# A decoder layer on one core: a front that multiplies before its norm, ten weight residues made by DMA, and a conv-out in split form throughout

## The chip, the core and the metric

The kernel runs on one core of a Trainium2 chip. The core has five engines that run beside each other and meet at semaphores: TensorE (PE in the profile; the loading of its weights, which overlaps the matmuls, is shown as PEld), VectorE (DVE), ScalarE (ACT), GpSimd (POOL) and SyncE (SP), which here only issues transfers; 16 DMA engines carry these. The metric is the device time of one execution in microseconds, lower is better.

## The reference

One layer of a trunk with sequence length 256, model width 1024, batch 1, all in float32:

```python
n = rmsnorm(x) * g_mix
z = n @ w_in                    # a, gate, q, k, v, index q, index k, index weights, two gate logits
u = a * sigmoid(gate)           # conv branch: causal depthwise convolution, 31 taps
u = causal_conv31(u) + conv_b
y_conv = silu(layernorm(u) * ln_g + ln_b) @ w_conv_out
y_attn = sparse_attention(q, k, v, index...) @ w_attn_out      # 8 heads, 64 keys of each query
h = x + (g_conv * y_conv + g_attn * y_attn) @ w_mix_out
h = h + cross_attention(rmsnorm(h), rmsnorm(mem))              # 4 heads, 256 memory tokens
h = h + square(relu(rmsnorm(h) @ w_ff1)) @ w_ff2               # width 4096
return rmsnorm(h) * g_final
```

Some 85 MB of weights pass through the core once.

## The kernel before

**Split products.** A product in float32 is made in one of two ways. *Native*: PE multiplies the float32 operands as they are, which appears in the trace as two matmul records for each matmul. *Split*: each operand is written as a high part, rounded to the type fp32r, and a low part, the rest (raw − high); three fp32r matmuls (`mm3`: high·high, high·low, low·high) replace one native product.

**The stream of weights.** The weights come in the fixed order `STREAM`, in chunks of 1 MB (128 partitions x 2048), two halves each. `load()` issues the next chunk on SP's queue into one of three `raw` buffers. For each half, `high` (line 174) has ACT copy the raw half to the high part (line 178), and its inner `low` has DVE subtract it to give the low part; when the low part of a chunk's second half is emitted, the next `load()` is issued, since the raw buffer then comes free. `highs` and `lows` have six buffers (`HALVES`). `weights(kind, i, half, kt)` hands out a prepared half; `split_ahead()`, called once for each half that is used, emits one more low part and one more high part. So the number of halves prepared ahead stays what it was. Chunks in `WHOLE` are used native and are never split: these are conv 0 and co 0. Chunks in `EARLY` have a buffer of their own: chunk 3 and co 0.

**The order** of each engine's instructions is written out by the program (a manual schedule): each engine runs its own in the order in which they were emitted. Work that is not tied to a product waits in generators (`chains`), which `tick()`, called after each half, moves on by one step each, and in `fill`, a list of taps of the convolution. `Counted` keeps a running estimate of PE's and DVE's work (`pe.total`, `dve.total`), and `tick` emits taps on DVE as long as its estimate is over 1 us behind PE's.

**The front** (lines 321 to 411). SP loads x in rows (`x_rm`, two loads), then the chunks conv 0, conv 1 and conv 2, the taps' weights `cw` and chunk 3. POOL's queue loads `vec`, a tile with all gains and biases. PE makes ten matmuls on zeros (`ps_warm`, line 350). ACT squares the rows with a sum, DVE and POOL make the scale of each row (POOL's `pow`), DVE multiplies, PE transposes to feature-major (`pt_n`), ACT and DVE multiply by the gain `g_mix` into `n_f`, and its high and low parts go to `n2`. conv 0 is native from `n_f`; everything later that takes n uses `n2`.

**The conv branch.** `conv_in(i)` makes two halves (gate and value of 128 channels), the sigmoid, the product `u`, and puts 30 taps of DVE on `fill`; `tap(t, s)` adds one. When a channel tile has its last tap, POOL adds it to `usum` (line 455), and the last of eight starts `layer_norm()` (line 595). This runs step by step at ticks: the mean over the channels by a matmul (`ps_mub`), squares, their sum (`ps_vr`), POOL's `pow`, the spread of the row scale (`ps_rsb`), then four multiplications on DVE and eight Silu on ACT over `acc`, and last the high and low parts of `acc`, two channel tiles at a tick (`parts_of`, into `u2`).

**From attention to the mix.** The products q, k, xk, xv and ao (attention out) are split; the heads run in chains. `form_b` makes one half after the other in the two banks `ps_mm`. After ao, the loop `while not normed: tick()` runs until the Silu is emitted; then co (conv out) follows. co 0 is native and reads `acc` itself, by `form_b_whole` (line 302) in two banks of `ps_acc`, in four steps with a tick behind each, during which the parts of `u2` are made; co 1 to 3 are split and use `u2`. `gated` (line 717) multiplies the result by its gate on DVE, adds the attention branch and makes the parts for mix. `form_b_late`, which other stages use, makes all but the last k tile of both halves first, then the last tile of both.

**The feed-forward.** `form_c_last("xo", ...)` ends the cross attention; `xo_residual` (line 912) makes the parts `ff_p`. Then `f1` and `f2` chunks alternate; f1 0 is made with `form_b_late`.

Line 77 is the helper through which all counted PE and DVE instructions are recorded.

Of the kernel before, what the change touches and what calls it, by code (L numbers as in the profile page):

```python
# [8 lines left out]
F32 = mybir.dt.float32  # L9
# [3 lines left out]
ALU = mybir.AluOpType  # L13
# [41 lines left out]
NK = 72  # L55
N_CHUNK = KT * S
HALVES = 6
EARLY = (3, STREAM.index(("co", 0)))
WHOLE = (("conv", 0), ("co", 0))


class Counted:
# [49 lines left out]
def block_kernel(ctx, tc, x, xt, mem, memt, wst, wki, vecs, convw, gout, out):  # L112
# [15 lines left out]
    def t8(name, dt=F32, shape=(P, KT, S)):  # L128
        return big.tile(list(shape), dt, tag="t8", bufs=12, name=name)

    def parts_t8(name, nkt=KT):
        return Parts([t8(f"{name}{c}", F32R, (P, 4, 2, S)) for c in range(nkt // 4)])
# [10 lines left out]
    def ps_acc(name):  # L143
        return bank("acc", 4, name)
# [9 lines left out]
    def load(parts=1):  # L154
        if nload[0] >= len(STREAM):
            return
        c = nload[0]
        nload[0] += 1
        key = STREAM[c]
        raw = t8(f"raw{c}", F32, (P, N_CHUNK)) if c in EARLY else raws.tile([P, N_CHUNK], F32, tag="raw", name=f"raw{c}")  # L160
        n = KT * NK if key[0] == "ki" else N_CHUNK
        src = wki if key[0] == "ki" else wst[INDEX[key]]
        for q in range(parts):
            ns = slice(q * n // parts, (q + 1) * n // parts)
            nc.sync.dma_start(raw[:, ns], src[:, ns])
        if key in WHOLE:
            whole[key] = raw.rearrange("p (k n) -> p k n", k=2 * KT)
            return
        parts = 1 if key[0] == "ki" else 2
        for q in range(parts):  # L170
            ns = slice(q * n // parts, (q + 1) * n // parts)
            high_jobs.append(lambda ns=ns, q=q, last=q == parts - 1: high(key, c, raw, ns, q, last))

    def high(key, c, raw, ns, q, last):
        n = ns.stop - ns.start
        hi = highs.tile([P, N_CHUNK // 2], F32R, tag="hi", name=f"hi{c}_{q}")[:, :n]
        lo = lows.tile([P, N_CHUNK // 2], F32R, tag="lo", name=f"lo{c}_{q}")[:, :n]
        act(hi, raw[:, ns], AF.Copy)  # L178

        def low():  # L180
            dve.tensor_tensor(out=lo, in0=raw[:, ns], in1=hi.bitcast(F32), op=ALU.subtract)
            prepared[(*key, q)] = (hi, lo)
            if last and c not in EARLY:
                load()

        low_jobs.append(low)
# [26 lines left out]
    def split_ahead():  # L213
        if not waiting[0]:
            split_low()
        split_high()

    def tick():
        for c in list(chains):
            if next(c, "end") == "end":  # L220
                chains.remove(c)
        while (len(fill) > 1 or (fill and (len(done) > 5 or nused[0] < 5))) and dve.total < pe.total - 1000:
            fill_one()
        dve.total = max(dve.total, pe.total - 2000)
# [18 lines left out]
    def split(hi, lo, src):  # L243
        act(hi, src, AF.Copy)
        dve.tensor_tensor(out=lo, in0=src, in1=hi.bitcast(F32), op=ALU.subtract)
# [53 lines left out]
            tick()  # L299
        held[0] = 1  # L300

    def form_b_whole(kind, i, x, after, cuts):

        w = whole[(kind, i)]
        banks = [ps_acc(f"ps_{kind}{i}{ct}")[:, :S] for ct in range(2)]
        for lo, hi in zip((0, *cuts), (*cuts, KT)):
            for ct in range(2):
                for kt in range(lo, hi):
                    pe.matmul(banks[ct], w[:, ct * KT + kt, :], x[:, kt, :], start=kt == 0, stop=kt == KT - 1)
            split_ahead()  # L310
            if hi == KT:
                load()
            tick()
        for ct in range(2):
            after(2 * i + ct, banks[ct])

    def copy_to(dst):
        return lambda ct, ps: act(dst[:, ct, :], ps, AF.Copy)


    x_rm = t8("x_rm", F32, (P, 2, D))
    for rb in range(2):
        nc.sync.dma_start(x_rm[:, rb, :], x[rb * P : (rb + 1) * P, :])
    vec = cst.tile([P, 72], F32, name="vec")
    nc.gpsimd.dma_start(vec, vecs)
    bgc, bga, cvb, lng, lnb, g_mix, g_mem, g_x, g_ffn = (vec[:, 8 * j : 8 * j + 8] for j in range(9))
    cw = cst.tile([P, KT, TAPS], F32, name="cw")
    for parts in (2, 2, 1):
        load(parts)
    nc.sync.dma_start(cw, convw.rearrange("p (k t) -> p k t", k=KT))  # L330
    load()
    zero = w2("zero")
    nc.vector.memset(zero, 0.0)
# [12 lines left out]
    nc.scalar.activation(half, half, AF.Sigmoid, bias=0.0, scale=0.0)  # L346
    nc.gpsimd.memset(half, -0.5)
    ps = ps_aux("ps_warm")
    for j in range(10):
        nc.tensor.matmul(ps, zero_r[:, :P], zero_r, start=True, stop=True)  # L350


# [5 lines left out]
    def row_square(src, rb, ss):  # L358
        junk = w2(f"junk_{src.name if hasattr(src, 'name') else ''}{rb}", BF16, (P, D))
        act(junk, src[:, rb, :], AF.Square, accum_out=ss[:, rb : rb + 1])  # L360
# [21 lines left out]


    n2 = parts_t8("n_p")
    n_f = t8("n_f")
    ss = small.tile([P, 2], F32, tag="ss", name="ss_n")
    ptn = [ps_acc(f"pt_n{c}") for c in range(4)]
    for rb in range(2):
        row_square(x_rm, rb, ss)
    for rb in range(2):  # L390
        ms = small.tile([P, 1], F32, tag="ms1", name=f"ms_n{rb}")
        dve.tensor_scalar(ms, ss[:, rb : rb + 1], 1.0 / D, EPS, ALU.mult, ALU.add)
        rs = small.tile([P, 1], F32, tag="rs1", name=f"rs_n{rb}")
        nc.gpsimd.tensor_tensor(out=rs, in0=ms, in1=half[:, 0:1], op=ALU.pow)
        dve.tensor_scalar(x_rm[:, rb, :], x_rm[:, rb, :], rs[:, 0:1], None, ALU.mult)
        for kt in range(KT):
            pe.transpose(ptn[kt // 2][:, (kt % 2) * S + rb * P : (kt % 2) * S + rb * P + P],
                         x_rm[:, rb, kt * P : kt * P + P], ident)
    for kt in range(KT):
        src = ptn[kt // 2][:, (kt % 2) * S : (kt % 2) * S + S]  # L400
        if kt % 2 == 1:
            dve.tensor_scalar(n_f[:, kt, :], src, g_mix[:, kt : kt + 1], None, ALU.mult)
        else:
            act(n_f[:, kt, :], src, AF.Copy, scale=g_mix[:, kt : kt + 1])
    for c in range(0, KT, 2):
        split(n2.high(c, 2), n2.low(c, 2), n_f[:, c : c + 2, :])
    split_high()
    split_low()
    split_high()
    pe.total = dve.total = 0.0  # L410


    mem2 = parts_t8("mem_p")
# [28 lines left out]
    def tap(t, s):  # L442
        def go():
            j = TAPS - 1 - s
            if s == 0:
                act(acc[:, t, :], u[:, t, :], AF.Identity, scale=cw[:, t, j : j + 1], bias=cvb[:, t : t + 1])
            else:
                dve.scalar_tensor_tensor(out=acc[:, t, s:], in0=u[:, t, : S - s], scalar=cw[:, t, j : j + 1],
                                         in1=acc[:, t, s:], op0=ALU.mult, op1=ALU.add)
            if s == TAPS - 1:  # L450
                done.append(t)
                if len(done) == KT:
                    start(layer_norm())
                if len(done) > 1:
                    nc.gpsimd.tensor_tensor(out=usum, in0=usum if len(done) > 2 else acc[:, done[0], :],
                                            in1=acc[:, t, :], op=ALU.add)
        return go

    def conv_tile(i, half):
        key = ("conv", i)  # L460
        w = weights("conv", i, half, KT) if key not in WHOLE else None
        split_ahead()
        ps = ps_mm(f"ps_conv{i}{half}")
        if w:
            tile_b(ps, w, n2)
        else:
            for kt in range(KT):
                pe.matmul(ps[:, :S], whole[key][:, half * KT + kt, :], n_f[:, kt, :], start=kt == 0, stop=kt == KT - 1)
        return ps

    def conv_in(i):
        psg = conv_tile(i, 0)
        sg = w2(f"sg{i}", F32, (P, S))
        act(sg, psg[:, :S], AF.Sigmoid)
        tick()
        psa = conv_tile(i, 1)
        dve.tensor_tensor(out=u[:, i, :], in0=psa[:, :S], in1=sg, op=ALU.mult)
        tick()
        tap(i, 0)()
        fill.append([tap(i, s) for s in range(1, TAPS)])  # L480
        if ("conv", i) in WHOLE:
            load()

    for i in range(4):
        conv_in(i)
        if i == 1:
            start(memory())


    qi_t = t8("qi_t", F32, (P, 4, S))  # L490
# [97 lines left out]
        form_a("v", hf, n2, v_rm, (1.0, 1.0))  # L588


    u2 = []

    normed = []

    def layer_norm():
        u2.append(parts_t8("u_p"))
# [25 lines left out]
        for c, cs in enumerate(pairs):  # L622
            dve.tensor_tensor(out=acc[:, cs, :], in0=acc[:, cs, :], in1=rsb, op=ALU.mult)
            for t in (2 * c, 2 * c + 1):
                act(acc[:, t, :], acc[:, t, :], AF.Silu, scale=lng[:, t : t + 1], bias=lnb[:, t : t + 1])
        normed.append(True)
        for c in range(4):
            yield
            parts_of(2 * c)
# [74 lines left out]
        form_b("ao", i, o2, copy_to(ya))  # L704
    while fill:
        fill_one()
    while not normed:
        tick()


    h_t = t8("h_t")
# [18 lines left out]

    gate_branch(0)
    for i in range(4):
        if i == 0:
            form_b_whole("co", i, acc, gated, (2, 4, 6))
        else:
            form_b("co", i, u2[0], gated)
    low_due.pop()()


# [386 lines left out]
```

## Time and profile before

| | |
|---|---|
| median of 3 runs | 516.89 us (516.72 to 516.94) |
| profiled execution | 516.86 us, its span 515.1 us |
| granted TensorE clock | 0.998 |
| PE busy | 504.3 us, 98% of the span |
| DVE, ACT, POOL busy | 419.4 us (81%), 286.9 us (56%), 19.2 us (4%) |
| DMA moved | 92.75 MB, mean 180 GB/s |

Rows of the profile read so: in a group of instructions, the line, engine and operation, out<-in with the shapes, the count, then busy time in all, mean ns of one, and the idle time of the engine before them with what ended it. In the timeline and in the chain, the first number is the start in us and the second the duration. In the list of waits: us in total, times, longest. In DMA issues: KB of each and the median time from issue to landing. `<-` in brackets names what released the waiting instruction.

### The profile page before, as it was taken

What the parts mean: (1) busy time and instruction counts of PE and PEld (TensorE: products, weight loads), DVE (VectorE), ACT (ScalarE), POOL (GpSimd) and SP (SyncE); (2) the same over time, 40 slices, a digit from 0 to 9 for tenths busy, and PEclk for the clock granted to TensorE, in tenths of its full rate; (3) what the DMA queues carried; (4) which work ended last, traced back from release to release, by engine and by line L of the source; (5) the groups of instructions that cost most, each with busy time, mean ns of one, the idle gap of its engine ahead of it and who ended that gap; (6) DMA issues with size and microseconds to landing.
All of it is one profiled execution on the core that took longest, in us unless ns stands there. A gap on an engine that the chain in (4) does not pass through costs nothing.

```text
span 515.1 us, 8515 instructions
## 1 busy us (share of the span) xinstructions
PE 504.3 (98%) x3354; PEld 463.1 (90%) x3354; DVE 419.4 (81%) x796; ACT 286.9 (56%) x489; POOL 19.2 (4%) x30
## 2 busy tenths in 40 slices
PE   7999999999999999999999999999999999999995
PEld 5999999999899999999999998988888888888884
DVE  4998999999988999999898976696766566666565
ACT  5666655546446666656655657565654454554442
POOL 2000000001001000021000000000000000000000
PEclk9999999999999999999999999999999999999999
DMA  8856435464552343454744541446445554445402
GB/s 317 359 187 236 155 122 205 174 225 183 194 216 102 144 164 118 155 224 161 275 143 155 207 184 44 181 165 242 164 169 220 221 207 163 164 174 219 181 1 81
DMA packets 14311, 92.75 MB, mean 180 GB/s; under 512 B 1584, under 2 KB 2480, under 8 KB 3776
## 3 DMA queue, kind: packets, MB, share of 16 engines
q1 hardware_dynamic: 13952, 91.85, 48.3%
q8 instruction: 26, 0.43, 0.3%
q10 hardware_dynamic: 288, 0.33, 0.2%
q14 instruction: 13, 0.11, 0.1%
q0 software_dynamic: 32, 0.04, 0.0%
HBM read 91.16 MB, written 1.05 MB: 179 GB/s over the span
## 4 chain that ended last, share of the span: by engine, by line
PE 95%; issue 1%; ACT 1%; DVE 1%; DMA 1%; POOL 0%; POOLq 0%; DVEq 0%; ACTq 0%
PE ps_f L77 17%; PE ps_ff L77 16%; PE ps_conv L77 9%; PE ps_co L77 5%; PE ps_ao L77 4%; PE ps_ga L77 4%; PE ps_gc L77 4%; PE ps_k L77 4%; PE ps_q L77 4%; PE ps_mix L77 4%; PE ps_v L77 4%; PE ps_xo L77 3%; PE ps_xq L77 2%; PE ps_qi L77 2%; PE ps_xk L77 2%; PE ps_xv L77 2%
## 5 line engine op out<-in xcount | busy, mean ns | idle before, releaser
L77 DVE TENSOR_TENSOR lo<-raw,hi 128x1024 fp32r<-128x1024 f32 x161 | 195.7, 1225 | 3.3 <-ACT hi L178 1.6
L178 ACT ACTIVATE hi<-raw 128x1024 fp32r<-128x1024 f32 x161 | 166.4, 1047 | 2.5 <-PE ps_v L77 2.5
L77 DVE SCALAR_TENSOR_TENSOR acc<-u,cw,acc 128x255 f32<-128x255 f32 (+27 forms) x240 | 100.6, 475 | 0.6
L77 PE MATMUL ps_f<-ff_p,hi 128*128 128x512 f32 x256 | 89.8, 396 | 0.0
L77 PE MATMUL ps_ff<-hi,fs 128*128 128x512 f32 (+1 forms) x256 | 80.8, 387 | 0.0
L77 PE MATMUL ps_f<-ff_p,lo 128*128 128x256 f32 x256 | 66.2, 279 | 0.0
L77 PEld LDWEIGHTS ps_ff<-hi,fs 128*128 128x128 f32 x256 | 47.9, 188 | 9.2
L77 PEld LDWEIGHTS ps_f<-ff_p,hi 128*128 128x128 f32 x256 | 46.8, 188 | 9.2
L77 DVE TENSOR_TENSOR ft<-ps_f,ft 128x256 f32<-128x256 f32 x32 | 13.6, 423 | 46.4 <-ACT ft L957 46.4
L77 PEld LDWEIGHTS ps_f<-ff_p,lo 128*128 128x128 f32 x256 | 48.2, 188 | 2.6
L957 ACT ACTIVATE ft<-ps_f 128x256 f32<-128x256 f32 x32 | 12.2, 380 | 66.9 <-PE ps_f L77 66.9
L77 PE MATMUL ps_ff<-lo,fs 128*128 128x512 f32 (+1 forms) x128 | 49.4, 386 | 0.0
L77 PE MATMUL ps_conv<-n_p,hi 128*128 128x256 f32 x224 | 41.0, 285 | 0.0
L77 PEld LDWEIGHTS ps_conv<-n_p,hi 128*128 128x128 f32 x224 | 34.9, 192 | 0.8 <-issue 0.7
L77 PE MATMUL ps_conv<-n_p,lo 128*128 128x256 f32 x112 | 31.7, 283 | 0.0
L77 PEld LDWEIGHTS ps_ff<-lo,fs 128*128 128x128 f32 x128 | 24.1, 188 | 4.9
L77 PE MATMUL ps_q<-n_p,hi 128*128 128x256 f32 x128 | 24.4, 291 | 0.0
L77 PE MATMUL ps_ao<-o_p,hi 128*128 128x256 f32 x128 | 23.5, 285 | 0.0
L77 PE MATMUL ps_k<-n_p,hi 128*128 128x256 f32 x128 | 23.4, 284 | 0.0
L77 PE MATMUL ps_gc<-n_p,hi 128*128 128x256 f32 x128 | 23.1, 283 | 0.0
L77 PE MATMUL ps_ga<-n_p,hi 128*128 128x256 f32 x128 | 23.1, 283 | 0.0
L77 PE MATMUL ps_mix<-mix_p,hi 128*128 128x512 f32 (+1 forms) x80 | 22.1, 350 | 0.0
(229 smaller groups left out, 1003.3 us busy)
## 6 DMA issues: line engine op xcount, KB each, us to landing
raw<-in_wst_dram SPq DMA_DIRECT2D x80, 1024.0 KB, 4.8
raw<-in_wst_dram SPq DMA_DIRECT2D x4, 512.0 KB, 7.7
x_rm<-in_x_dram SPq DMA_DIRECT2D x2, 512.0 KB, 3.9
mem_rm<-in_mem_dram SPq DMA_DIRECT2D x1, 1024.0 KB, 9.0
mem_t<-in_memt_dram SPq DMA_DIRECT2D x1, 1024.0 KB, 11.0
h_t<-in_xt_dram SPq DMA_DIRECT2D x1, 1024.0 KB, 6.9
out_dram<-hg SPq DMA_DIRECT2D x4, 176.0 KB, 2.2
g_out<-in_gout_dram SPq DMA_DIRECT2D x1, 512.0 KB, 7.0
```

Source lines behind the costliest of these rows:

```text
L77: return fn(*args, **kwargs)
L178: act(hi, raw[:, ns], AF.Copy)
L957: act(t, ps[:, S:], AF.Copy)
```

## The change

It has three parts.

1. **The front.** x is loaded feature-major (`x_t`, two loads of four k tiles, the second behind the first half of conv 0). `xg` is x times the gain, not yet normed: two of the eight k tiles on ACT, six on DVE. conv 0 and conv 1 are native from `xg` in four `ps_acc` banks (`conv_in_first`). The squares of x are summed on ACT and DVE; `row_scale` makes the row scale with matmuls (`ps_n`) amid conv 0, spreads it (`rsb_n`) behind conv 0, and makes the normed `n_f` and the parts `n2` on DVE and ACT. The scale is put on the results of the two native chunks afterwards: the gate is multiplied by `rsb`, goes through the sigmoid, and is multiplied by `rsb` again. `cw` is loaded behind the second chunk, not the third. The matmuls on zeros are six instead of ten, and the planner starts behind this front with `pe.total = 0` and `dve.total = 2000` where both were 0 ahead of conv 0.
2. **Ten low parts by DMA.** For the second halves of the chunks 8, 11, ... 35 (the last is ao 0), ACT writes −high to the low part and a DMA on POOL's queue adds the raw half to it, in place of DVE's subtraction.
3. **co 0 is split** like the others and uses `u2`, by `form_b_late`; `form_b_whole` goes, and the loop before co runs until the whole chain of `layer_norm`, its parts included, has been emitted.

```diff
-EARLY = (3, STREAM.index(("co", 0)))
-WHOLE = (("conv", 0), ("co", 0))
+EARLY = (3,)
+WHOLE = (("conv", 0), ("conv", 1))
...
             nc.sync.dma_start(raw[:, ns], src[:, ns])
+            if c == 0 and q == 0:
+                nc.sync.dma_start(x_t[:, 4:8, :], xt[:, 4:8, :])
...
+    def low_by_dma(key, c, q):
+        return q == 1 and c % 3 == 2 and 8 <= c < STREAM.index(("ao", 1))
...
         act(hi, raw[:, ns], AF.Copy)
+        by_dma = low_by_dma(key, c, q)
+        if by_dma:
+            act(lo, hi.bitcast(F32), AF.Copy, scale=-1.0)
 
         def low():
-            dve.tensor_tensor(out=lo, in0=raw[:, ns], in1=hi.bitcast(F32), op=ALU.subtract)
+            if by_dma:
+                nc.gpsimd.dma_start(lo.bitcast(F32), raw[:, ns], accum_op=ALU.add)
+            else:
+                dve.tensor_tensor(out=lo, in0=raw[:, ns], in1=hi.bitcast(F32), op=ALU.subtract)
...
-    x_rm = t8("x_rm", F32, (P, 2, D))
-    for rb in range(2):
-        nc.sync.dma_start(x_rm[:, rb, :], x[rb * P : (rb + 1) * P, :])
+    x_t = t8("x_t")
     vec = cst.tile([P, 72], F32, name="vec")
     nc.gpsimd.dma_start(vec, vecs)
...
-    for parts in (2, 2, 1):
+    nc.sync.dma_start(x_t[:, 0:4, :], xt[:, 0:4, :])
+    for parts in (2, 1):
         load(parts)
     nc.sync.dma_start(cw, convw.rearrange("p (k t) -> p k t", k=KT))
     load()
+    load()
...
-    for j in range(10):
+    for j in range(6):
         nc.tensor.matmul(ps, zero_r[:, :P], zero_r, start=True, stop=True)
...
+    for kt in range(KT):
+        gain(kt, None if kt in (0, 2) else dve)
+    for hf in range(2):
+        act(n_f[:, 4 * hf : 4 * hf + 4, :], x_t[:, 4 * hf : 4 * hf + 4, :], AF.Square)
+    for n in (4, 2, 1):
+        dve.tensor_tensor(out=n_f[:, :n, :], in0=n_f[:, :n, :], in1=n_f[:, n : 2 * n, :], op=ALU.add)
+
+    def row_scale():
+        rs = rsqrt(n_f[:, 0, :], "n")
+        yield
+        act(rsb, spread(rs, "rsb_n"), AF.Copy)
+        yield
+        for c in range(0, KT + 2, 2):
+            if c < KT:
+                dve.tensor_tensor(out=n_f[:, c : c + 2, :], in0=xg[:, c : c + 2, :],
+                                  in1=rsb.unsqueeze(1).to_broadcast([P, 2, S]), op=ALU.mult)
+                act(n2.high(c, 2), n_f[:, c : c + 2, :], AF.Copy)
+            if c > 0:
+                dve.tensor_tensor(out=n2.low(c - 2, 2), in0=n_f[:, c - 2 : c, :], in1=n2.high(c - 2, 2).bitcast(F32),
+                                  op=ALU.subtract)
+            if c == 2:
+                split_high()
+            if c == 4:
+                split_low()
...
+    def conv_in_first():
+        scaling, banks = row_scale(), []
+        for i in range(2):
+            for half in range(2):
+                ps = ps_acc(f"ps_conv{i}{half}")[:, :S]
+                banks.append(ps)
+                for kt in range(KT):
+                    pe.matmul(ps, whole[("conv", i)][:, half * KT + kt, :], xg[:, kt, :], start=kt == 0,
+                              stop=kt == KT - 1)
+                    if kt == KT // 2 - 1 and i == 0 and half == 1:
+                        next(scaling)
...
+        for i in range(2):
+            psg, psa = banks[2 * i : 2 * i + 2]
+            sg = w2(f"sg{i}", F32, (P, S))
+            dve.tensor_tensor(out=sg, in0=psg, in1=rsb, op=ALU.mult)
+            act(sg, sg, AF.Sigmoid)
+            dve.tensor_tensor(out=sg, in0=sg, in1=rsb, op=ALU.mult)
+            gated_linear(i, psa, sg)
+
+    conv_in_first()
+    split_low()
+    pe.total = 0.0
+    dve.total = 2000.0
...
-    while not normed:
-        tick()
+    finish(norms[0])
...
     for i in range(4):
-        if i == 0:
-            form_b_whole("co", i, acc, gated, (2, 4, 6))
-        else:
-            form_b("co", i, u2[0], gated)
+        (form_b_late if i == 0 else form_b)("co", i, u2[0], gated)
```

More of the change, by code (lines that the diff above doesn't have):

```diff
@@ L300, in form_b_late @@
         held[0] = 1
[L302 to L312, printed above, removed]
-            tick()
-        for ct in range(2):
-            after(2 * i + ct, banks[ct])
     def copy_to(dst):
         return lambda ct, ps: act(dst[:, ct, :], ps, AF.Copy)
-    x_rm = t8("x_rm", F32, (P, 2, D))
-    for rb in range(2):
-        nc.sync.dma_start(x_rm[:, rb, :], x[rb * P : (rb + 1) * P, :])
+    x_t = t8("x_t")
     vec = cst.tile([P, 72], F32, name="vec")
@@ L384, in block_kernel @@
     n2 = parts_t8("n_p")
+    xg = t8("xg")
     n_f = t8("n_f")
[L386 to L398, printed above, removed]
@@ L399, in block_kernel @@
-    for kt in range(KT):
-        src = ptn[kt // 2][:, (kt % 2) * S : (kt % 2) * S + S]
-        if kt % 2 == 1:
-            dve.tensor_scalar(n_f[:, kt, :], src, g_mix[:, kt : kt + 1], None, ALU.mult)
-        else:
[L404 to L410, printed above, removed]
+    rsb = w2("rsb", F32, (P, S))
@@ new lines, in gain @@
+    def gain(kt, engine):
+        if engine is dve:
+            dve.tensor_scalar(xg[:, kt, :], x_t[:, kt, :], g_mix[:, kt : kt + 1], None, ALU.mult)
+        else:
+            act(xg[:, kt, :], x_t[:, kt, :], AF.Copy, scale=g_mix[:, kt : kt + 1])
+    for kt in range(KT):
+        gain(kt, None if kt in (0, 2) else dve)
[3 more added lines that the diff above has]
+        dve.tensor_tensor(out=n_f[:, :n, :], in0=n_f[:, :n, :], in1=n_f[:, n : 2 * n, :], op=ALU.add)
@@ new lines, in row_scale @@
+    def row_scale():
[15 more added lines that the diff above has]
+                split_low()
+        split_high()
+        split_low()
+        split_high()
+        yield
@@ L452, in go @@
                 if len(done) == KT:
-                    start(layer_norm())
+                    norms.append(start(layer_norm()))
                 if len(done) > 1:
@@ L459, in conv_tile @@
     def conv_tile(i, half):
-        key = ("conv", i)
-        w = weights("conv", i, half, KT) if key not in WHOLE else None
+        w = weights("conv", i, half, KT)
         split_ahead()
         ps = ps_mm(f"ps_conv{i}{half}")
[L464 to L468, printed above, removed]
+        tile_b(ps, w, n2)
         return ps
@@ L476, in conv_in, with gated_linear @@
         psa = conv_tile(i, 1)
-        dve.tensor_tensor(out=u[:, i, :], in0=psa[:, :S], in1=sg, op=ALU.mult)
-        tick()
+        gated_linear(i, psa[:, :S], sg)
+    def gated_linear(i, ps, sg):
+        dve.tensor_tensor(out=u[:, i, :], in0=ps, in1=sg, op=ALU.mult)
+        if ("conv", i) not in WHOLE:
+            tick()
         tap(i, 0)()
         fill.append([tap(i, s) for s in range(1, TAPS)])
-        if ("conv", i) in WHOLE:
-            load()
-    for i in range(4):
+    def conv_in_first():
[9 more added lines that the diff above has]
+                        next(scaling)
+                if half == 1:
+                    load()
+                if i == 0 and half == 1:
+                    next(scaling)
+                    next(scaling)
+        for i in range(2):
[6 more added lines that the diff above has]
+    conv_in_first()
+    split_low()
+    pe.total = 0.0
+    dve.total = 2000.0
+    start(memory())
+    for i in range(2, 4):
         conv_in(i)
-        if i == 1:
-            start(memory())
     qi_t = t8("qi_t", F32, (P, 4, S))
@@ L588, in block_kernel @@
         form_a("v", hf, n2, v_rm, (1.0, 1.0))
-    u2 = []
-    normed = []
+    u2, norms = [], []
     def layer_norm():
@@ L625, in layer_norm @@
                 act(acc[:, t, :], acc[:, t, :], AF.Silu, scale=lng[:, t : t + 1], bias=lnb[:, t : t + 1])
-        normed.append(True)
         for c in range(4):
@@ L706, in block_kernel @@
         fill_one()
-    while not normed:
-        tick()
+    finish(norms[0])
     h_t = t8("h_t")
@@ L732, in block_kernel @@
     for i in range(4):
-        if i == 0:
-            form_b_whole("co", i, acc, gated, (2, 4, 6))
-        else:
-            form_b("co", i, u2[0], gated)
+        (form_b_late if i == 0 else form_b)("co", i, u2[0], gated)
     low_due.pop()()
```

## The prediction

> **What bounds the kernel now.** I read four views in this order: busy time by engine, PE's waits, the chain of waits in order of time, and then the timeline around each place that the change touches.
>
> ```profile
> PE 504.3 (98%) x3354; PEld 463.1 (90%) x3354; DVE 419.4 (81%) x796; ACT 286.9 (56%) x489; POOL 19.2 (4%) x30
> ```
> ```profile
> core 0 of [0], span 515.1 us
> engine line waited for: us in total, times, longest us
> PE ps_warm L350 <- DVE zero_r L335: 1.9, 1, 1.9
> PE pt_n L77 <- DVE ms_n L77: 1.3, 1, 1.3
> PE ps_xo L77 <- ACT xptr L853: 0.8, 1, 0.8
> PE pt_n L77 <- DVE x_rm L77: 0.4, 1, 0.4
> ```
>
> PE is busy 504.3 of 515.1 us, and its whole list of waits is 4.4 us, of which 3.6 (all but ps_xo's 0.8) lie ahead of the first useful matmul. So an edit pays only if it takes matmul time off PE or moves the first matmul forward, and it costs as soon as it makes PE wait. DVE at 81% and ACT at 56% are covers: work taken off them is worth nothing by itself. The profiled run took 516.86 us, 1.8 more than its span, against a median of 516.89; I sum in the span and carry the result over unchanged. Differences under 0.2%, about 1 us, can't be told from no change.
>
> **The front.**
>
> ```profile
> 0.74 3.51 DMA x_rm<-in_x_dram
> ```
> ```profile
> 1.24 0.75 POOL L325 DMA_DIRECT2D vec<-in_vecs_dram  x1 [0.79 <-POOLq L1117]
> ...
> 9.65 7.26 PE L77 MATMUL ps_conv<-n_f,raw 128*128 128x256 f32 x32
> ...
> 16.56 0.58 PE L77 MATMUL ps_conv<-n_p,hi 128*128 128x256 f32 x2
> ```
> ```profile
> vec<-in_vecs_dram POOLq DMA_DIRECT2D x1, 36.0 KB, 5.5
> ```
> ```profile
> L380 ACT ACTIVATE mem_p<-mem_t,vec 128x256 fp32r<-128x256 f32 x8 | 4.0, 501 | 0.0
> ```
>
> Today the norm of x (squares, power, scaling, two rounds of transposes) runs ahead of the first matmul at 9.65. The change drops the transposes and the wait for the norm: PE may start once x_t and the gains in vec are there. x_t's first half takes x_rm's place in the queue (0.74 + 3.51 = 4.25); the weights follow in the same order and volume. But vec lands only at 1.24 + 5.5 = 6.74, and now the first gain waits for it; one gain is like the mem_p row, 0.50. So PE starts at about 7.25, 2.4 us earlier.
>
> What it starts with is dearer. A native fp32 chunk took 16.56 − 9.65 = 6.91 us; a split chunk of 48 matmuls takes 5.75 (the ps_ao x48 row below). Before, chunk 2 began at 16.56 + 5.75 = 22.31. After, it begins at 7.25 + 2 × 6.91 + 0.34 + 0.22 (the sums and the spread of the row scale, priced by the ps_vr and ps_rsb rows below) = 21.63. **Front: −0.7.** The split of the first weights and of n, and the four scaled gates, run on ACT and DVE beside 14 us of native matmuls. Bounds: were vec as quick as x_rm (3.5 instead of 5.5), −2.7; were the four gates and the parts of n late for chunk 2, nearest row the 0.4 that PE waited for x_rm, −0.3.
>
> The warm-up shrinks from ten matmuls to six, and then PE idles for some 2.8 us:
>
> ```profile
> L350 PE MATMUL ps_warm<-zero_r x10: 389/628/796, 1.9 to 5.4; 128*128 128x512 f32 x10
> ```
>
> The slowest of the ten lasted 796 ns, the quickest 389: the early ones ran at about half speed, although the granted clock in the windows reads 1.00. If six aren't enough, the first matmuls of conv run at half speed for about as long as the warm-up did, 3.5 us, and do 1.7 us less. I take zero, as PE is then busy again without a gap; the 1.7 stays in the range. The Trainium skill ("TensorE: Matmul & The Clock Gate", Part 1, What's actually happening) says that the full clock comes after about 3.4 us of sustained work and goes after an idle window; six matmuls at the slow rate are shorter than that, so by this page, as an estimate, the front would lose the 1.7 us and the sum below would be that much higher. The row agrees that the first matmuls are slow; when the clock falls back no run here shows.
>
> **Conv-out all split, and the norm behind it.**
>
> ```profile
> 219.80 5.49 PE ps_xv L77 x24
> 225.29 11.51 PE ps_ao L77 x96
> 236.81 0.43 PE ps_mub L77 x2
> 237.24 5.75 PE ps_ao L77 x48
> 242.99 0.34 PE ps_vr L77 x4
> 243.33 2.97 PE ps_ao L77 x24
> 246.30 0.22 PE ps_rsb L77 x2
> 246.52 2.87 PE ps_ao L77 x24
> 249.39 24.18 PE ps_co L77 x176
> ```
>
> Three split chunks of co are 3 × 5.75 = 17.25; the native one is 24.18 − 17.25 = 6.93. Splitting it saves 1.18. Its two results now lie in the two ordinary banks, which chunk 1 can reuse only after the first gated eviction (a few tenths, taken as 0.2). **co: −1.0.**
>
> The native chunk was also a cover. It needed acc after Silu, not its split parts, and used other banks than ao. In the changed program mub stands behind the first 24 ao matmuls, vr behind 72 and rsb behind 96, with 96 still to come. So the burst that follows rsb now falls in the middle of ao:
>
> ```profile
> 248.13 4.03 ACT L625 ACTIVATE acc<-acc,vec 128x256 f32<-128x256 f32 x8
> ...
> 253.02 0.36 ACT L318 ACTIVATE ya<-ps_ao 128x256 f32<-128x256 f32 x1
> ```
> ```profile
> 248.96 1.22 DVE L77 TENSOR_TENSOR lo<-raw,hi 128x1024 fp32r<-128x1024 f32 x1
> ```
>
> From rsb's start R (246.30) the next ya eviction ends at R + 7.1 (253.02 + 0.36). With two ps_mm banks, ao half 6 needs the bank that this eviction frees; at three halves of 2.88 behind, PE arrives about R + 6.6: 0.5 late. Half 5 needs a low part that DVE makes behind the four multiplications, R + 3.9 (248.96 + 1.22), against R + 3.3 in PE's order: 0.6. **ao: +1.1.** In exchange the parts of u are ready before co wants them (12 us after rsb, against four rounds of about 2.2). Bounds: 0 if the next half's weights happen to be done; all of the 4.0 of Silu if ACT serves nothing between.
>
> **Ten low parts by an adding DMA.** Ten second halves from chunk 8 on get −hi from ACT, and a DMA on POOL's queue adds raw to it.
>
> ```profile
> L77 DVE TENSOR_TENSOR lo<-raw,hi 128x1024 fp32r<-128x1024 f32 x160 | 194.9, 1228 | 3.3 <-ACT hi L178 1.6
> L178 ACT ACTIVATE hi<-raw 128x1024 fp32r<-128x1024 f32 x160 | 165.8, 1050 | 2.5 <-PE ps_v L77 2.5
> ```
>
> DVE is spared 10 × 1.23 = 12.3 us and spends them on the taps, so the norm comes earlier; ACT gets 10 × 1.05 = 10.5, which its 44% of idle time covers. On PE's path none of it counts unless a part is late. The first halves are prepared three ahead, 3 × 2.88 = 8.6 us; hi, −hi and one eviction take about 2.5 of it on ACT, so a DMA has some 6 us. How long it takes the trace doesn't show. Nearest rows: vec, the only transfer of that queue, 5.5 for 36 KB; x_rm's load of 512 KB, 3.5. The loads of weights fill less than half of the DMA engines' time:
>
> ```profile
> q1 hardware_dynamic: 13952, 91.85, 48.3%
> ```
>
> I take 5.5, as the same queue, so nine are hidden; at 7 each would lose about 1 us, 9 in all. The raw buffer is freed by the landing instead of by DVE, and SP's next load stands behind it; with the weights three chunks ahead and those 48.3% in the queue table, that costs nothing. The Trainium skill ("DMA: Bandwidth & Descriptors", Anatomy of one DMA) puts such a transfer at 2.0 us + bytes / 436 GB/s, 3.2 us here as an estimate; all ten would then be hidden with 3 us to spare. The vec row, 5.5 for 36 KB, speaks against it; it was issued among crowded loads.
>
> One is not hidden. The tenth, for ao half 1, is issued on POOL behind the additions of usum, and these wait for the last tap:
>
> ```profile
> 222.33 1.94 POOL L455 TENSOR_TENSOR usum<-usum,acc 128x256 f32<-128x256 f32 x1 [20.85 <-DVE acc L77]
> 224.69 0.80 POOL L455 TENSOR_TENSOR usum<-usum,acc 128x256 f32<-128x256 f32 x1 [0.42 <-DVE acc L77]
> 234.40 1.56 POOL L455 TENSOR_TENSOR usum<-usum,acc 128x256 f32<-128x256 f32 x1 [8.91 <-ACT ya L318]
> ```
> ```profile
> L77 DVE SCALAR_TENSOR_TENSOR acc<-u,cw,acc 128x255 f32<-128x255 f32 (+27 forms) x240 | 100.6, 475 | 0.6
> ```
>
> In the changed order the last tap is emitted ahead of the last xv half, which is half of the ps_xv row: 225.29 − 2.75 − 0.7 = 221.8. With two to five taps of 0.475 still queued then, and a sum of 0.8 to 1.9, the sum ends between 223.6 and 226.1. With 4.5 to 5.5 for the DMA (between x_rm's row and vec's, nearer to vec's) it lands at 228.1 to 231.6; ao half 1 starts at 225.29 − 0.7 + 2.88 = 227.5 and wants the part 0.2 later. Late by 0.4 to 3.9; I take 1.3, near the early end, because DVE has been relieved by nine parts. **+1.3.**
>
> **f1.** Preparing one half ahead less (co's native chunk used no prepared halves, a split one uses two) is felt where DVE is blocked:
>
> ```profile
> 329.71 16.78 PE ps_f L77 x96
> ```
> ```profile
> 330.35 1.66 DVE L77 SCALAR_TENSOR_TENSOR ff_p<-h_t,vec,ff_p 128x256 fp32r<-128x256 f32 x4
> 332.37 1.23 DVE L77 TENSOR_TENSOR lo<-raw,hi 128x1024 fp32r<-128x1024 f32 x1 [0.35 <-ACT hi L178]
> ```
>
> The lo of f1's second half now stands behind the last ff_p parts, 332.01 + 1.2 = 333.2; PE, which starts f1 at 329.7 and holds seven eighths of its first half (2.5 us), wants it at 332.2. **f1: +1.0.** Bounds 0 and 2.
>
> **The sum.** −0.7 − 1.0 + 1.1 + 1.3 + 1.0 = +1.7: 516.9 + 1.7 = **518.6 us**.
>
> **The rivals.** *Faster:* the covers hold. If vec lands as the loads around it do, the front gives 1.9, co 1.0, and if the DMA of ao half 1 goes out before the last sum and the ao and f1 halves are ready, nothing is lost: 516.9 − 2.9 = 514.0; with one of the three stalls, 515. For it: PE's short list of waits, so the planner's leads are generous. Against it: the orders of ACT, DVE and POOL, which put the named instructions behind each other. It decides at vec landing before 6.4 and fewer than two stalls. *Much slower:* the adding DMA takes more than the 6 us of its window. Each us beyond costs nine; at 6.5 that is 4 to 5, and with the sum 523. It decides from 6.1 on. For it: 5.5 for a fourteenth of the bytes, and the source and the target are both read. Against it: vec was issued while the queues were full. *A cold clock:* six warm-up matmuls and the pause leave the first 3.5 us of conv at half speed; the sum becomes 518.6 + 1.7 = 520.3, as by the page named at the warm-up. For it: the slow early matmuls of the warm-up row. Against it: the change of speed came within those ten. *The norm doesn't come forward:* if the taps still end where they do now, co's parts come at 2.2 us a pair while PE eats a pair in 0.7 each; 4 × 1.5 − 1.0 = 5 us slower, 522. The order of DVE, with mub behind 24 instead of 96 ao matmuls, speaks against it.
>
> **How the numbers follow.** Chances: the sum, slower by 0.2% to 4 us, 0.41, of which 0.10 with the cold clock; much slower by the DMAs 0.11, by a norm that stays 0.03; faster, 0.37; within 0.2%, where one stall less stands against the gains, 0.08. The forecast is the end of the first case's sum. The range reaches from 514.4 (the faster case without its last half us) to 525 (a DMA of 6.7 us); about a tenth is left out on each side. The likeliest case alone goes from 518.0 to 521. Slower is 0.41 + 0.11 + 0.03 = 0.55.
>
> **What would show it.** In the changed profile: first conv matmul at 7.25 and chunk 2 at 21.6; vec as what the first gains wait for; ps_co as 23.2; in PE's waits, ao on ACT's ya and on lo, f1 on lo, and ao half 1 on a DMA of lo, with the times above; and the adding DMA's row in the DMA issues, at 5.5 or less. I am wrong if PE's waits stay at 4 us in all, or if a wait for DMA appears in q, k or ga.

## The result

| | before | after |
|---|---|---|
| median | 516.83 us (516.72 to 516.94, 4 runs) | 537.64 us (536.53 to 540.3, 4 runs) |
| profiled execution, its span | 516.86, 515.1 | 540.3, 538.5 |
| PE busy | 504.3 (98%) | 511.9 (95%) |

The ratio is 1.041 (95% interval 1.0382 to 1.0439): 20.8 us slower where 1.7 was forecast. The profiled execution is the longest of the four, so its stages add up to more, 23.4. Two executions of later runs are left out as slow: one of b_dma (836.6 us, granted clock 0.56) and one of b_co (2836.6 us).

First the page of the changed kernel: the engines' busy time, and the engine shares of the chain that ended last.

```profile
PE 511.9 (95%) x3340; PEld 466.1 (87%) x3340; DVE 409.9 (76%) x796; ACT 296.7 (55%) x496; POOL 27.1 (5%) x39
...
PE 71%; DVE 12%; DMA 6%; ACT 5%; issue 4%; POOL 0%; POOLq 0%; DVEq 0%; ACTq 0%
```

The chain lay on PE for 95% of the span, now for 71%. DVE has 9.5 us less to do and ACT 9.8 more; what grew is PE's waiting for them. The twelve longest rows of the changed kernel's list of PE's waits say where:

```profile
PE ps_conv L77 <- ACT xg L390: 4.3, 1, 4.3
PE ps_ao L77 <- DMA lo<-raw: 3.0, 1, 3.0
PE ps_gc L77 <- DMA lo<-raw: 2.5, 1, 2.5
PE ps_warm L347 <- DVE zero_r L332: 1.9, 1, 1.9
PE ps_xo L77 <- ACT ox_p L256: 1.5, 1, 1.5
PE ps_conv L77 <- ACT sg L480: 1.3, 1, 1.3
PE ps_xq L77 <- DVE lo L77: 1.1, 1, 1.1
PE ps_ao L77 <- DVE lo L77: 0.9, 2, 0.6
PE ps_f L77 <- DVE lo L77: 0.8, 1, 0.8
PE ps_xo L77 <- ACT xptr L882: 0.8, 1, 0.8
PE ps_mix L77 <- DVE lo L77: 0.7, 1, 0.7
PE ps_v L77 <- DMA lo<-raw: 0.6, 1, 0.6
```

Only ps_warm's 1.9 and xptr's 0.8 stood in the list before. The twelve add to 19.4 us, against 4.4, and that isn't all, since a pause of PE has a second price. The windows of the changed kernel around three of them (columns: window, its length, busy time and count of PE, PEld, DVE, ACT, POOL, granted clock, DMA share, GB/s):

```profile
100.00:104.00 4.00, 1.58 (x14) 1.38 (x12) 4.00 (x11) 1.42 (x2) 0.45 (x1) 1.00 0.76 164
104.00:108.00 4.00, 3.93 (x32) 3.93 (x33) 4.00 (x8) 0.99 (x2) 0.00 (x0) 1.00 0.69 242
239.00:243.00 4.00, 1.08 (x9) 1.09 (x10) 3.80 (x7) 2.82 (x5) 0.00 (x0) 1.00 0.66 121
243.00:247.00 4.00, 4.00 (x24) 4.00 (x23) 1.94 (x3) 1.65 (x3) 0.00 (x0) 0.57 0.88 295
342.00:346.00 4.00, 2.42 (x16) 1.99 (x15) 0.44 (x2) 1.33 (x2) 0.00 (x0) 0.96 0.98 393
346.00:349.00 3.00, 3.00 (x16) 3.00 (x16) 1.13 (x2) 0.91 (x2) 0.00 (x0) 0.50 0.15 57
```

Behind the last two of these pauses, in ao and in xo, the granted clock falls to a half, for 3.41 us each in the clock's record, which costs PE another 1.7 each. Behind the first, in gc, it stays at 1.00, although PE waited 2.5 us there and only 1.5 in xo. So the length of a pause doesn't settle by itself whether the clock falls; what does isn't shown here. The Trainium skill ("TensorE: Matmul & The Clock Gate", Part 1, What's actually happening) gives a free-running window of 3413 ns; the length agrees, but the two pauses that were followed by half speed, 1.7 and 3.3 us from the last matmul's issue, were not as long as a whole idle window.

Where each stage's first matmul stands, from the timelines of the two and of two kernels that are explained below:

| stage | before | after | late by | a_lead | late by | b_dma_co_ao | late by |
|---|---|---|---|---|---|---|---|
| qi | 34.01 | 39.47 | 5.5 | 40.72 | 6.7 | 33.89 | −0.1 |
| gc | 75.56 | 81.02 | 5.5 | 82.28 | 6.7 | 75.44 | −0.1 |
| ga | 98.61 | 106.81 | 8.2 | 105.41 | 6.8 | 98.87 | 0.3 |
| xk | 198.16 | 207.23 | 9.1 | 204.97 | 6.8 | 198.42 | 0.3 |
| mix | 273.40 | 289.21 | 15.8 | 280.94 | 7.5 | 273.40 | 0.0 |
| xo | 315.44 | 334.19 | 18.8 | 322.97 | 7.5 | 315.43 | 0.0 |
| f1 | 329.55 | 351.53 | 22.0 | 337.08 | 7.5 | 329.55 | 0.0 |
| end | 515.08 | 538.49 | 23.4 | 522.79 | 7.7 | 515.26 | 0.2 |

So a quarter was lost ahead of qi, and the rest in many places down to f1, where the prediction had three stalls.

### The profile page after: what moved, and what is told of

Same layout as the page of the kernel before. It is cut to its first block, busy times and chain, and to the rows that moved or that the text cites. A ratio compares the mean times of both kernels' runs of the same rounds, so it can differ in the third digit from the quotient of the medians.

```text
span 538.5 us, 8503 instructions
## 1 busy us (share of the span) xinstructions
PE 511.9 (95%) x3340; PEld 466.1 (87%) x3340; DVE 409.9 (76%) x796; ACT 296.7 (55%) x496; POOL 27.1 (5%) x39
## 4 chain that ended last, share of the span: by engine, by line
PE 71%; DVE 12%; DMA 6%; ACT 5%; issue 4%; POOL 0%; POOLq 0%; DVEq 0%; ACTq 0%
PE ps_f L77 16%; PE ps_ff L77 15%; PE ps_co L77 4%; PE ps_ga L77 4%; PE ps_k L77 4%; PE ps_q L77 4%; PE ps_mix L77 4%; DVE acc L77 3%; DMA lo<-raw 3%; DVE lo L77 3%; PE ps_ao L77 3%; PE ps_conv L77 3%; PE ps_v L77 3%; PE ps_qi L77 2%; DMA raw<-in_wst_dram 2%
## 5 line engine op out<-in xcount | busy, mean ns | idle before, releaser
L77 DVE TENSOR_TENSOR lo<-raw,hi 128x1024 fp32r<-128x1024 f32 x151 | 182.7, 1222 | 3.1 <-ACT hi L184 2.7
L77 DVE SCALAR_TENSOR_TENSOR acc<-u,cw,acc 128x254 f32<-128x254 f32 (+29 forms) x240 | 98.5, 467 | 0.4
L77 PE MATMUL ps_conv<-n_p,hi 128*128 128x256 f32 x192 | 35.4, 286 | 1.3 <-ACT sg L480 1.3
L77 PEld LDWEIGHTS ps_conv<-n_p,hi 128*128 128x128 f32 x192 | 29.9, 191 | 2.3 <-ACT sg L480 1.5
L77 PE MATMUL ps_conv<-n_p,lo 128*128 128x256 f32 x96 | 27.1, 283 | 0.0
L77 PE MATMUL ps_ao<-o_p,hi 128*128 128x256 f32 x128 | 25.2, 297 | 0.3 <-ACT ya L315 0.3
L77 PE MATMUL ps_co<-u_p,hi 128*128 128x256 f32 x128 | 23.3, 284 | 0.2 <-DVE gc_t L77 0.2
L77 PE MATMUL ps_k<-n_p,hi 128*128 128x256 f32 x128 | 23.4, 284 | 0.0
```

Of the source, the lines that this page charges most:

```text
L77: return fn(*args, **kwargs)
```

## The experiments

What the many places share is the lead, the number of halves prepared ahead. I counted it in the order in which the program emits its work: from chunk 2 on the kernel before keeps three highs and two lows ahead of the half in use; the changed one keeps two and one, and from ao 1 on none of the lows. The reason is that conv 0's native halves called `split_ahead` without using a prepared half, which the new front no longer does; and that the low part which a step of the norm leaves out was made good by native co 0, which called it four times. All theories below start from here.

**a_lead**, the lead put back:

```diff
     conv_in_first()
     split_low()
+    split_high()
+    split_low()
```

> The changed kernel with one more high part and one more low part prepared ahead of chunk 2 (an extra split_high and split_low behind the first two chunks), so that three highs and two lows lie ahead instead of two and one, and one low ahead instead of none from attention out on. Theory L (the lead is what was lost): the DMA stalls in gc (2.7), v (0.9) and ao (3.2) and the waits for low parts in mix, xq, xo and f1 (1.3, 1.4, 3.2, 1.1) mostly go: 537.6 - 11 = 525 to 528; the front keeps its 5.5. Theory D (the adding DMAs are too slow in themselves, whatever the lead): gc, v and ao keep their waits for the DMA, 533 to 537. Theory M (weights landing late because raw buffers are freed late): no change, 536 to 539.

Measured: 523.2 us (522.15 to 524.57), ratio 1.0116 (1.0095 to 1.0137): 14.4 us won by two lines, more than theory L's range of 525 to 528 gave. PE's waits in a_lead:

```profile
PE ps_conv L77 <- ACT xg L390: 3.5, 1, 3.5
PE ps_conv L77 <- ACT sg L480: 2.2, 1, 2.2
PE ps_warm L347 <- DVE zero_r L332: 1.9, 1, 1.9
PE ps_ao L77 <- ACT ya L315: 1.2, 1, 1.2
PE ps_xo L77 <- ACT xptr L884: 0.8, 1, 0.8
PE ps_co L77 <- DVE gc_t L77: 0.2, 1, 0.2
```

Every wait for a low part or for its DMA is gone, although the DMAs became no quicker. Their landing in the changed kernel and in a_lead, from the view of the tile lo:

```profile
DMA to landing us min/median/max: 4.6/4.7/8.5
```
```profile
DMA to landing us min/median/max: 4.5/5.8/8.4
```

The longest is that of gc's last half in both. The chain of the changed kernel shows it on PE's path; there it was wanted at 101.3 already, 5.7 us behind its issue. In a_lead the same transfer is issued at 94.02 and wanted at 102.4 (gc's start at 82.28 and seven halves of 2.88), 8.4 behind its issue: one half more.

```profile
95.56 8.47 DMA lo<-raw
...
104.07 2.90 PE ps_gc L77 x22
```

**a_tail**, one low part more ahead of conv-out, nothing earlier touched:

```diff
     finish(norms[0])
+    split_low()
```

> The changed kernel with one more low part made right ahead of conv-out, so that from there on one low part lies ahead instead of none; nothing ahead of conv-out is touched. Theory L: the waits behind it (mix 1.3, xq 1.4, xo 3.2 with the slow clock that follows the pause, f1 1.1) go: 537.6 - 6 = 531 to 532. Theory M (late loads or something else in these stages): at most 1 us, 536 to 538.

Measured: 531.69 us (531.67 to 531.89), 6.0 less, as theory L had it. So one low part is worth 6 us in mix, xq, xo and f1 together. How a late low part reaches xo, in the chain of the changed kernel: with no low ahead, a raw buffer is freed late, its load comes late, ACT waits for it with a high part, and ox_p, which PE needs, stands behind that high part on ACT.

```profile
338.27 4.84 DMA raw<-in_wst_dram
...
343.20 1.06 ACT hi L184
344.25 0.28 ACT ox_p L256
...
345.03 5.23 PE ps_xo L77 x29
```

The list of waits calls this "ACT ox_p"; the chain names the load.

**a_nodma**, the changed kernel with all low parts on DVE:

```diff
-        return q == 1 and c % 3 == 2 and 8 <= c < STREAM.index(("ao", 1))
+        return False
```

> The changed kernel with the ten low parts made by DVE again, all else as it is; the planner then keeps one low part ahead from attention out on. Theory L: the three DMA stalls (6.8) and the waits in mix to f1 (7) go, and DVE has 11 us more to do ahead of the norm, which makes ao or conv-out wait by 0 to 5: 524 to 529. Theory D (DMAs alone): 537.6 - 6.8 = 530 to 531, with the waits behind conv-out still there.

Measured: 533.0 us (532.06 to 533.66), above what either theory gave. The waits for the DMAs and those from mix to f1 are gone (the latter need not be the DMAs' doing, since in this program one low part stays ahead from ao on), but in their place stand the largest rows of its list of PE's waits:

```profile
PE ps_vr L77 <- DVE vs L77: 5.3, 1, 5.3
PE ps_conv L77 <- ACT xg L390: 3.4, 1, 3.4
PE ps_co L77 <- DVE u_p L77: 2.9, 1, 2.9
```

and the clock's record has 10.2 us at half speed behind them. Without the DMAs the norm comes too late. Most of that seems to be the new front's doing, as DVE can start the taps of conv 0 only when its u is there. The rows for it, first before (timeline), then after (chain):

```profile
17.15 0.42 DVE L77 TENSOR_TENSOR u<-ps_conv,sg 128x256 f32<-128x256 f32 x1
```
```profile
29.35 0.44 DVE u L77
```

Twelve us later, on an engine that is full until the norm: this is what the DMAs' 12 us pay for. The support for it is b_co below, which has the old front and no DMAs and loses only some 3 us.

**b_dma, b_co, b_dma_co**: parts of the change on the kernel before, with its old front and full lead: the DMAs alone, split co 0 alone, both. The edits are those of the diff above.

> The kernel before with the ten low parts by the adding DMA and nothing else. Its lead is three highs and two lows. Theory L (a DMA of 4.5 to 8.5 us is hidden by that lead): no wait for a DMA of lo on PE, DVE about 12 us less busy, the time the same as before: 516 to 517.5. Theory D (the DMAs cost whatever the lead): waits in gc and ao as in the changed kernel, 2.5 + 3: 521 to 524.

> The kernel before with conv-out 0 split and nothing else: all low parts on DVE, the old front. Theory N (DVE is full until the norm, so the native chunk was the norm's cover): ps_vr waits for DVE and co for the parts of u, about 5.3 + 2.9 + 1.0 as in the changed kernel without DMAs, and the clock falls for a while: 516.8 - 1 + 9 to 14 = 525 to 530. Rival (the native chunk only cost matmul time): 516.8 - 1 = 515.5 to 516.

> The kernel before with the DMAs and the split conv-out, but with the old front: the change without its front. Theory L with N: the DMAs bring the norm forward, co is 0.8 to 1.0 shorter, ao waits 1.2 to 1.5 for ya behind the eight Silu: 516.8 + 0.5 = 516.5 to 518. Then the front is what stays of the change with its lead mended (523.2 - 517). Rival (the later stages lose by themselves): 519 to 523.

Measured: b_dma 519.4 us (ratio 1.0044, 1.0028 to 1.0061), b_co 520.4 (1.0062, 1.0045 to 1.0079), b_dma_co 518.67 (1.0034, 1.0023 to 1.0046). b_co's wait for the parts of u is 1.5, where theory N had 9 to 14 for all such waits, so its size was wrong with this front; its rival, a gain of 1, was wrong too. b_dma missed both theories: no 2.5 + 3, but no zero either. b_dma_co lies 0.7 above the range of L with N and just under its rival's; its trace has the wait for ya of 1.2 that L with N named. Against a_lead's 523.2 it puts the price of the new front, with the lead mended, at 4.5 us.

**b_dma_co_ao, b_dma_ao, b_dma_again**: why the DMAs cost some 2.5 by themselves. Theory B is that they bring the norm forward into ao, where the eight Silu then hold ya. The edit gives ao four banks instead of two:

```diff
-        form_b("ao", i, o2, copy_to(ya))
+        form_b("ao", i, o2, copy_to(ya), ps_acc)
```

> The kernel before with the DMAs, the split conv-out and attention out in the four ps_acc banks, with the old front. Theory B: 518.7 - 1.2 to 1.4 = 517.3, 516.8 to 517.8. Rival: 518.7 still.

> The kernel before with the ten DMAs, conv-out 0 still native, and attention out in the four ps_acc banks. Theory B (the DMAs cost nothing themselves; they bring the norm into attention out, where ya's eviction waits behind the eight Silu): 519.4 - 1.4 = 518.0, and 0.8 above b_dma_co_ao (the native chunk). Theory D (waits for the DMAs themselves): 519.4 still.

> The same program as b_dma, for its trace. Theory B: 519.4; PE's list has ao waiting for ya by 1.2 to 1.4 and no wait for a DMA of lo. Theory D: a wait for lo's DMA of 1 to 2.5.

Measured: b_dma_co_ao 517.09 (ratio 1.0005, 0.9996 to 1.0014), b_dma_ao 517.94 (1.002, 1.0011 to 1.003), b_dma_again 519.27. The three times are as theory B had them; the row that goes is this one of b_dma_again's list of PE's waits, and no wait for a DMA stands in any of the three:

```profile
PE ps_ao L77 <- ACT ya L328: 1.2, 1, 1.2
```

The four banks take away 1.3 to 1.5 of the 2.5. b_dma_ao still lies 1.2 above the kernel before, and no row of its list of waits accounts for that; this part of the DMAs' price, or of what they move, stays open. b_dma_co_ao is the best version of these parts and equals the kernel before; none beats it.

**a_front, a_lead_warm, a_gates, a_gates_warm, a_gates_warm_ao**: the front. First vec on SP's queue, ahead of x, and ten warm-up matmuls:

```diff
-    nc.gpsimd.dma_start(vec, vecs)
+    nc.sync.dma_start(vec, vecs)
...
-    for j in range(6):
+    for j in range(10):
```

> The changed kernel with vec as the first load of SP's queue and ten matmuls on zeros instead of six. Theory F (late gains and the cold clock make the front): vec lands at 4 instead of 8.6, the first matmul starts at 6.5 to 7.3 instead of 9.2 and at full speed, which gives 1.9 to 2.7 and 2.6: 537.6 - 4.8 = 532 to 533.5, chunk 2 at 21 to 22 instead of 26.6. Rival G (the gates and the parts of n on DVE and ACT set chunk 2 and 3, not the first matmul): PE starts earlier but waits for n's parts, at most 2 us gained, 535.5 or more.

Measured: 537.65 us (535.19 to 540.0): nothing gained, inside rival G's range. vec now lands 1.9 us after its issue, yet the first wait only changes its name. From a_front's DMA issues and its list of PE's waits:

```profile
vec<-in_vecs_dram SPq DMA_DIRECT2D x1, 36.0 KB, 1.9
```
```profile
PE ps_conv L77 <- DMA raw<-in_wst_dram: 2.3, 1, 2.3
```

The first weights land at 8.4, so PE starts at 8.5 at best; and the ten matmuls, which end at 6.2, don't keep the clock: its record has half speed from 9.16 on for 3.41 us. Theory F's late gains were wrong as a bound, and its cold clock wasn't removed by this edit.

Then 24 matmuls on zeros on top of a_lead:

```diff
-    for j in range(6):
+    for j in range(24):
```

> The changed kernel with the mended lead and 24 matmuls on zeros instead of 6, so that PE is busy until the first weights and gains are there. Theory F (cold clock): the first 5 us of conv run at full speed, 2.5 us saved: 523.2 - 2.5 = 520 to 521.5. Rival G: what is won is waited for at the gates of the first two chunks (the wait of conv for the sigmoid, 2.2, grows): 522 to 523.5.

Measured: 523.35 us (523.1 to 523.39), within a_lead's runs. The warm-up ended at 9.6, 1.3 us later than a_lead's first product began, and chunk 2 began at 23.77 instead of 25.02; the wait for the gates, 2.3, and half speed behind it stayed. As a test of the clock it is inconclusive.

Then, again on top of a_lead, the gate of conv 1 behind chunk 2 (a_gates), with it 18 matmuls on zeros (a_gates_warm), and then ao in four banks as well (a_gates_warm_ao):

```diff
-        for i in range(2):
+        def gates(i):
...
-    conv_in_first()
+    gates = conv_in_first()
+    gates(0)
...
     for i in range(2, 4):
         conv_in(i)
+        if i == 2:
+            gates(1)
```

> The changed kernel with the mended lead, and with the gate of conv 1 made behind chunk 2 instead of ahead of it; the gate of conv 0 stays where it is. Theory F2 (the front's largest loss is ACT and DVE passing the two gates to and fro while chunk 2's own gate waits on ACT, and the slow clock that follows that pause): the wait of 2.2 and the 1.7 of half-speed clock go: 523.2 - 3.9 = 519 to 520.5. Rival (the parts of n are late for chunk 2 and 3, whatever the gates do): 522 to 523.5.

> The same with 18 matmuls on zeros instead of 6, which reach to about 8.2, where the first weights land. Theory F: the first matmuls run at full speed and nothing behind gives it back now: 2.5 less than a_gates, 516.5 to 518. Rival (the clock isn't held by matmuls on zeros, or the later steps of the front take it back): same as a_gates.

> The same, and attention out in the four ps_acc banks instead of the two ps_mm. Theory B (ao waits for its bank, since ya's eviction stands behind eight Silu on ACT): the wait of 1.2 goes, 515.5 to 517. Rival (ao waits for a low or high part as well): no gain.

Measured: 522.44 (521.25 to 522.73), 520.29 (519.96 to 520.32) and 518.8 us (518.63 to 519.09). In a_gates the wait for the gates falls from 2.2 to 0.3 and no half speed follows; the profiled run is 2.4 us shorter than a_lead's, but the median only 0.8, and the intervals of the ratios overlap (1.0095 to 1.0137, 1.0087 to 1.0121). The median lies in the rival's range, and two of a_lead's own runs took 522.2. So it is shown that the wait goes with this edit; that it saves time isn't. The warm-up is worth some 2.1 us between the medians, near theory F's 2.5; the time itself lies above F's range, which counted on more from a_gates. The same 24 records of the first conv matmuls, in the chain of the changed kernel and of a_gates_warm:

```profile
9.15 8.12 PE ps_conv L77 x24
```
```profile
8.71 5.23 PE ps_conv L77 x24
```

The four banks give 1.5, and the wait for ya is gone as theory B had it, though the time stays above B's range. With all this the changed kernel still stands 2.0 us (518.8 against 516.8) above the kernel before. In its trace qi starts at 35.4, 1.4 later than before, and `ps_mub` waits 0.8 for POOL's `usum`.

## Why the prediction was wrong, step by step

1. **What bounds the kernel.** Right: all that was lost are waits of PE. But the text took the short list of waits as a sign of generous leads. A list of waits doesn't show how near to late the work behind it is.
2. **The front, −0.7; measured +5.5.** Three terms failed. PE started at 9.15, not 7.25 (1.9): vec took 7.3 in this profile instead of 5.5, and a_front shows that with vec early the first weights hold PE until 8.5. The prediction let the weights "follow in the same order and volume" and never asked when they land. The clock, taken at zero, cost 2.9 (8.12 against 5.23 for the same 24 records). The rival with the cold clock came about, and the page named there pointed the right way; the 1.7 that the prediction gave it was too little, since 2.9 lost at half speed means some 5.8 us of half speed (an estimate), where it took 3.5. The gates and the parts of n, priced at 0 to 0.4, made PE wait 1.4 between two matmuls, as chunk 2's own gate stood on ACT behind the gates of both native chunks. (The list of waits gives this one as 1.3.) 1.9 + 2.9 + 1.4 = 6.2, the whole error of this step.
3. **co, −1.0.** Right in sign and near in size: −0.7 in a_lead (257.48 to 280.94, 23.46 against 24.18).
4. **ao, +1.1.** The sum came out, its two terms didn't. The prediction had 0.5 for ya's bank and 0.6 for a low part. The changed kernel waits 0.3 and 0.9 for them; with the lead restored, a_lead waits 1.2 for ya alone, gone with four banks.
5. **Nine DMAs hidden.** A landing of 5.5 was taken; the median was 4.7, so the value was fair and the rival of slow DMAs didn't come about. What failed was taking one value for all, and the window: the prediction counted the halves as prepared three ahead, where the changed program keeps two. One landing took 8.47 and made PE wait 2.5 in gc, and one of 4.57 still made it wait 0.6 in v, issued only at 134.38 behind work of ACT. That the window in gc was 5.7, close to the prediction's "some 6 us", is luck: with three ahead, in a_lead, it was 8.4. With the kernel before's lead all ten are hidden.
6. **The tenth, behind usum, +1.3.** Its place was right. The last sum ended at 237.3, the transfer at 241.9, and PE waited 3.0, inside the bounds; the slow clock behind it added 1.7, which wasn't in the sum.
7. **The lead, "one half ahead less", +1.0 in f1.** This is the step that failed most. The prediction saw only the loss at conv-out, and f1's wait is there (0.8), but it priced that loss at one place only, where DVE looked blocked. The other loss, from chunk 2 on, which the new front brings, it put at nothing, without a reason. a_tail shows 6.0 for one low part behind ao, and a_lead 14.4 for the whole lead, which also made the waits of steps 5 and 6 what they were. The faster case needed covers that hold, and fewer were left than its text supposed; the much slower one priced the DMAs at nine late ones, where two were late and the low parts of DVE did the rest.

## What to carry to other kernels

When a change alters how many prepared pieces lie ahead of the consumer, count that lead stage by stage in both programs, and price its loss at every stage whose longest producer delay exceeds the new lead, not only at the first that shows. A stage that used nothing of the queue but advanced it was a cover, and two lines here gave it back. A pause of the matmul engine can cost more than its length: here 1.7 us more behind two of the changed kernel's longer pauses, and nothing more behind a third.

## What the runs showed of the hardware

An adding DMA of 512 KB within SBUF, from POOL's queue, landed after 4.5 us at the least (a_lead) and 8.5 at the most (the changed kernel). The Trainium skill ("DMA: Bandwidth & Descriptors", Anatomy of one DMA) makes it 3.2 as an estimate; no run came near that. A load of 36 KB landed after 4.8 (b_dma_co) to 7.3 us (the changed kernel) from POOL's queue and after 1.9 as the first of SP's (a_front). In the changed kernel the clock fell to a half for 3.41 us behind PE's waits of 3.0 us in ao and 1.5 in xo, and did not fall behind one of 2.5 in gc.
